# Attention's scores all beside the projections, its last values between the state space's scans, and GpSimd's products given to VectorE

## The chip, the cores and the metric

The kernel runs on one core of a Trainium2 chip. The metric is the time of one execution on the device, in microseconds, as the median of several runs.

A core has engines that each run their own instructions in order and wait for one another by semaphores: TensorE (PE, matrix products and transposes, into eight PSUM banks), VectorE (DVE, elementwise work, reductions and scans), ScalarE (ACT, activations and copies), GpSimd (POOL) and SyncE (SP, which here issues most DMAs).

## The reference

One decoder layer on a sequence of 1024 tokens with 1024 channels, in float32. Three parts follow each other, each with an RMSNorm ahead and behind, and a shift, scale and gate from a conditioning vector: half a SwiGLU step, token mixing, half a SwiGLU step. The change touches mixing alone:

```python
def sliding_window_attention(q, k, v, sinks):      # 8 query heads, 2 key heads, blocks of 128
    ...                                            # each block reads its own and the previous key block
    scores = einsum('bnqkgd,bnjkd->bnkgqj', qb, kk) * HEAD_DIM ** -0.5
    scores = where(valid, scores + bias, -inf)
    m = maximum(max(scores, axis=-1), sink)
    p = exp(scores - m)
    p = p / (sum(p, axis=-1) + exp(sink - m))
    out = einsum('bnkgqj,bnjkd->bnqkgd', p, vv)
    ...
def s5_ssm(u, a_re, a_im, log_step, b_re, b_im, c_re, c_im, d_skip, w_glu, b_glu):
    ...
    _, states = lax.associative_scan(combine, (a, bu), axis=1)   # complex diagonal state
    y = real(einsum('bsgp,ghp->bsgh', states, c_mat)) + u * d_skip
    y = gelu(y)
    y = y * sigmoid(y @ w_glu + b_glu)
    ...
```

The normed input is projected by w_in to q, k, v (attention, 512 channels) and u (state space, 512 channels). The outputs of both, each normed, are projected together by w_out.

## The kernel before, in words

Products of float32 matrices are made of three matmuls in a shorter format (`mm3`, L72 to L76): the high part of each side by the high part of the other, and the high parts by the low ones. `split` (L67 to L70) makes the parts: a cast by ACT (L69) and a subtraction by VectorE (L70).

PSUM banks of the mixing stage are handed out in turn, `b0` to `b7` (`mb`): an instruction that writes a bank waits until the last reader of what stood there before is done. The high and low parts of the transposed probabilities rotate over `h0` to `h7` (`o_rot`). In the listings below the names are tiles without that number, and behind them the number of the use: `b_1133` is a tile of the program, here in some bank.

The whole body stands in a context that gives the order of each engine's instructions by a schedule of its own (`TileContext(nc, schedule_with_timeline_sim=True)`), so the order on an engine follows the order in the code loosely. On an engine, the order is then fixed.

Mixing has twelve projection steps s = 0 to 11: four by `project` (the q, k and v columns that are left), then eight by `project_u`, one for each block of 128 tokens, 24 matmuls each (L919 to L921) and four copies by ACT (L923). Between them attention is threaded in: `at(n)` does three pieces of attention that belong to three blocks, `at_values(n - 3)`, `at_turn(n - 2)` and `at_scores(n)`. The table `AT` (L702) says behind which steps an `at` stands.

- `at_scores(t)`: two pairs of PSUM banks get the products of queries and keys (L831). VectorE adds the bias and takes the maximum (L841), ACT exponentiates (L848, L850, eight heads), VectorE sums, inverts and scales (L851, L852, L854, eight rows of work).
- `at_turn(t)`: TensorE transposes the probabilities (L865), `split` makes high and low parts from the banks (L69, L70).
- `at_values(t)`: `mm3` with the values (two groups of six matmuls, one group of three for block 0), ACT squares and copies the result out of its bank (L880, L882), VectorE sums the squares (L884), a matmul with ones sums over the heads (L886), VectorE copies that (L887).

Then u is transposed to `ug` (L949, copies by ACT at L950), and the state space runs over four groups of channels, q = 0 to 3. `ss_load(q)` fetches operands. `ss_state(q)` makes the input products (L968, 16 matmuls), scales and sums them on VectorE (L976 to L981), runs two scans along time (L982, L983), and turns the states back by three elementwise products and sums each for the real part (on VectorE, L993 to L995) and the imaginary one (the same lines, on POOL). The scans' decay factors are laid out by a POOL copy (L973). `ss_out(q)` makes the outputs (L1006, L1010), a Gelu on ACT (L1013), and transposes back (L1017, L1019). `out_a(t)` (L1038) is attention's share of w_out's product for block t, 24 matmuls. It needs `mix_a`, the split attention output, and the scale `rstd_a` (L1047). `more(n)` does one further `at(n)` between the state space's steps, and after the last one loads w_out's operands and makes `mix_a`.

Of the kernel before, what the change touches and what calls it, by code (L numbers as in the profile page):

```python
# [11 lines left out]
F32R = mybir.dt.float32r  # L12
# [3 lines left out]
MUL, ADD, SUB, MAX, MIN = ALU.mult, ALU.add, ALU.subtract, ALU.max, ALU.min  # L16

P = 128
D = 1024
NK = 8  # L20
NT = 8
# [9 lines left out]
def tile_layer(ctx: ExitStack, tc: tile.TileContext, a: dict, out: bass.AP, stage: str = "all"):  # L31
    nc = tc.nc
    pe, act, dve, pool, sp = nc.tensor, nc.scalar, nc.vector, nc.gpsimd, nc.sync
# [10 lines left out]
    def slot(tag, shape, dt=F32):  # L44
        uid[0] += 1
        return sb.tile([P] + list(shape), dt, tag=tag, name=f"{tag}_{uid[0]}")
# [5 lines left out]
    def small(n, name):  # L52
        uid[0] += 1
        return sm.tile([P, n], F32, tag=f"s_{name}_{n}", name=f"s{uid[0]}")
# [13 lines left out]
    def split(hi, lo, src, eng=dve):  # L68
        act.copy(hi, src)  # L69
        eng.tensor_tensor(lo, src, hi.bitcast(F32), op=SUB)  # L70
# [38 lines left out]
    r8 = cp.tile([P, 16], F32, name="r8")  # L109
    rstd_a, rstd_s, ss_a = (cp.tile([P, 8], F32, name=x) for x in ("rstd_a", "rstd_s", "ss_a"))  # L110
# [27 lines left out]
    def rsqrt(v, n):  # L138

        s, y = small(n, "rss"), small(n, "rsy")  # L140
        act.activation(s, v, AF.Sqrt)
        dve.reciprocal(y, s)
        dve.scalar_tensor_tensor(s, y, -0.5, y, op0=MUL, op1=MUL)
        dve.tensor_tensor(s, s, v, op=MUL)
        dve.scalar_tensor_tensor(y, s, 1.5, y, op0=ADD, op1=MUL)
        return y

    def rstd_of(ss, n, count):

        v = small(n, "rsv")  # L150
        dve.tensor_scalar(v, ss, 1.0 / count, EPS, op0=MUL, op1=ADD)
        return rsqrt(v, n)
# [546 lines left out]
        return todo  # L699


    AT = (1, 1, 0, 1, 0, 1, 0, 1, 0, 1, 0, 1)  # L702


    mb = Rot(*names("b", *range(8)))
# [48 lines left out]
    def mix(hm, st, st_u, late, shares, todo, start):  # L754
# [62 lines left out]
        ag = [slot(f"r{m}", [D]) for m in range(4)]  # L817
# [71 lines left out]
        def ss_load(q):  # L889
            e = slot(f"q{q % 2}", [4, 2, P])  # L890
            tw = slot(f"q{2 + q % 2}", [2, 512])
            f = slot(f"q{4 + q % 2}", [2, 4, P])
            tt = slot(f"q{6 + q % 2}", [8, P])
            sp.dma_start(e, e_d[q])
            sp.dma_start(tw, tw_d[q])
            for j in range(8):
                src = kp_d[q * P : (q + 1) * P, 112 - 16 * j : 240 - 16 * j].rearrange("(g h) w -> h g w", g=8)
                sp.dma_start(tt[16 * j : 16 * j + 16], src)
            sp.dma_start(f, f_d[q])
            B[q] = dict(e=e, tw=tw, f=f, t=tt)  # L900


        def at(n):

            if 3 <= n < NT + 3:
                at_values(n - 3)
            if 2 <= n < NT + 2:
                at_turn(n - 2)
            if n < NT:
                at_scores(n)  # L910
# [14 lines left out]
        n = 0  # L925
        for s in range(12):
# [6 lines left out]
            else:  # L933
# [3 lines left out]
                project_u(s - 4)  # L937
            if AT[s]:
                at(n)
# [19 lines left out]
        W = [slot(t, [2, 512]) for t in names("a", 4, 5, 6)]  # L959

        def ss_state(q):
            b = B[q]
            pp = [bank(mb(), [4, P]) for _ in range(2)]
            for g in range(4):
                for gp in range(2):
                    rows = slice(64 * gp, 64 * gp + 64)
                    for ri in range(2):
                        pe.matmul(pp[ri][rows, g, :], b["e"][:, g, ri, rows], ug[q][:, 2 * g + gp, :], start=True, stop=True)  # L968
            cs, sn = b["tw"][:, 0], b["tw"][:, 1]
            ir, ii = (p_.rearrange("p g c -> p (g c)") for p_ in pp)  # L970
            w1, w2, w3, w4, w5, w6 = (x[:, i] for x in W for i in range(2))
            dc = w5.rearrange("p (g c) -> p g c", g=4)
            pool.tensor_copy(dc, r8[:, 4 * q : 4 * q + 4].unsqueeze(2).broadcast_to([P, 4, P]))  # L973
            pool.memset(dc[:, :, 0], 0.0)

            dve.tensor_tensor(w1, ir, cs, op=MUL)  # L976
            dve.tensor_tensor(w2, ii, sn, op=MUL)
            dve.tensor_tensor(w1, w1, w2, op=ADD)
            dve.tensor_tensor(w3, ii, cs, op=MUL)
            dve.tensor_tensor(w4, ir, sn, op=MUL)  # L980
            dve.tensor_tensor(w3, w3, w4, op=SUB)  # L981
            dve.tensor_tensor_scan(w2, w5, w1, 0.0, op0=MUL, op1=ADD)  # L982
            dve.tensor_tensor_scan(w4, w5, w3, 0.0, op0=MUL, op1=ADD)  # L983

            hh = slot(("a8", "a9")[q % 2], [2, 4, P])
            hr, hi = hh[:, 0], hh[:, 1]

            def v3(x):
                return x.rearrange("p (g c) -> p g c", g=4)[:, :, 0 : P - 1]

            for dst, (p0, p1), op in ((hr, (cs, sn), SUB), (hi, (sn, cs), ADD)):
                eng, u1, u3 = (dve, w1, w3) if dst is hr else (pool, w5, w6)
                eng.tensor_tensor(u1, w2, p0, op=MUL)  # L993
                eng.tensor_tensor(u3, w4, p1, op=MUL)
                eng.tensor_tensor(dst[:, :, 1:P], v3(u1), v3(u3), op=op)  # L995
                pool.memset(dst[:, :, 0], 0.0)
            b["h"] = (hr, hi)

        def ss_out(q):
            b = B.pop(q)  # L1000
            yn = slot("a7", [8, P])
            py = [bank(mb(), [4, P]) for _ in range(2)]
            for g in range(4):
                for gp in range(2):
                    gr = 2 * g + gp
                    pe.matmul(py[gp][:, g, :], ug[q][:, gr, :], b["t"][:, gr, :], start=True, stop=False)  # L1006
                for ri in range(2):
                    for gp in range(2):
                        rows = slice(64 * gp, 64 * gp + 64)
                        pe.matmul(py[gp][:, g, :], b["h"][ri][rows, g, :], b["f"][rows, ri, g, :], start=False, stop=ri == 1)  # L1010
            for gp in range(2):
                dst = yn.rearrange("p i (g b h) -> p b g i h", g=4, b=2)[:, gp]
                act.activation(dst, py[gp].rearrange("p g (i h) -> p g i h", i=8), AF.Copy if stage == "ypre" else AF.Gelu_apprx_tanh)  # L1013
            for ih in range(2):
                pt = bank(mb(), [4, P])
                for i in range(4):
                    pe.transpose(pt[:, i, :], yn[:, 4 * ih + i, :], ident)  # L1017
                dst = y_t[q].rearrange("p (t i l) -> p t i l", t=8, i=8)[:, :, 4 * ih : 4 * ih + 4, :]
                act.copy(dst, pt.rearrange("p i (t l) -> p t i l", t=8))  # L1019
# [10 lines left out]
        def out_a(t):  # L1030
            acc.append(slot(("r1", "r2", "r3", "a14", "a15", "a4", "a5", "a6")[t], [D]))
            tk = slice(t * P, (t + 1) * P)
            for dh in range(2):
                dk = slice(dh * 512, dh * 512 + 512)
                pb = bank(mb())
                for m in range(4):
                    mm3(pb, mix_a[0][m][:, tk], mix_a[1][m][:, tk], wo[m][0][:, dk], wo[m][1][:, dk], m == 0, m == 3)
                dve.tensor_scalar(acc[t][:, dk], pb, rstd_a[:, t : t + 1], None, op0=MUL)  # L1038

        wo, mix_a = [], []  # L1040

        def more(n):
            if n < NT + 3:
                at(n)
            if n == NT + 2:
                late.load(1)
                dve.tensor_copy(rstd_a, rstd_of(ss_a, 8, 512))  # L1047
                mix_a.extend([slot(f"a{16 + 4 * i + m}", [D], F32R) for m in range(4)] for i in range(2))
                for m in range(4):
                    split(mix_a[0][m], mix_a[1][m], ag[m])  # L1050
                wo.extend(late.get(i) for i in range(4))
            return n + 1

        ss_load(1)
        n = more(n)
        ss_state(0)
        n = more(n)
        ss_state(1)
        n = more(n)
        ss_out(0)  # L1060
        ss_load(2)
        n = more(n)
        ss_state(2)
        n = more(n)
        ss_out(1)
        ss_load(3)
        while n < NT + 3:
            n = more(n)
        ss_state(3)
        out_a(0)  # L1070
        out_a(1)
        ss_out(2)
        y_split(0)
        y_split(1)
        out_a(2)
        out_a(3)
        ss_out(3)
        for t in range(4, 8):
            out_a(t)
        y_split(2)  # L1080
        y_split(3)
# [32 lines left out]
        wo = [shares.get(i) for i in range(4)]  # L1114
# [306 lines left out]
    w1 = Weights(a["w1_gu"], names("a", 4, 5, 6, 7), dve)  # L1421
# [109 lines left out]
    ins, us, late, shares = mix_streams()  # L1531
# [147 lines left out]
```

## Time and profile before

| | before |
|---|---|
| median of 3 runs | 1693.89 us (1691.98 to 1694.91) |
| profiled execution | 1698.31 us, span 1696.4 us |
| mean granted TensorE clock | 0.987 |
| PE busy | 1650.6 us, 97% of the span |
| VectorE, ACT, POOL busy | 74%, 47%, 6% of the span |

The span is the profiled part of one execution, the 1698.31 us are its whole time. "Busy" counts an engine's instructions without waits. The clock is the share of full speed that TensorE was granted; a matmul at half clock counts as busy twice as long. Mixing takes up the stretch from about 700 to 1050 us.

### The profile page before, as it was taken

The numbers are of one execution on the slowest core, as the hardware profiler recorded it, in microseconds if no ns is written. First come the engines' busy times: TensorE is split into PE (matmuls) and PEld (weight loads), VectorE is DVE, ScalarE is ACT, GpSimd is POOL, SyncE is SP. The second block draws the span as 40 slices with busy tenths as digits, with TensorE's granted clock in tenths as the row PEclk, the third lists the DMA queues.
The fourth block names the chain that finished last, engine by engine and source line by source line (L and its number), as shares of the span: only waits on it lengthen the run. The fifth ranks groups of instructions, "written<-read, shape, count | busy, mean of one in ns | idle before, by whom it ended". The sixth has DMA issues, their size and how long they took to land.

```text
span 1696.4 us, 22121 instructions
## 1 busy us (share of the span) xinstructions
PE 1650.6 (97%) x7669; PEld 1354.7 (80%) x7669; DVE 1254.8 (74%) x2407; ACT 802.4 (47%) x1650; POOL 107.8 (6%) x139
## 2 busy tenths in 40 slices
PE   5999999999999999999989998999999999999998
PEld 4888888787788888888767876878888888888886
DVE  7999997788869668746489368877665666679585
ACT  4633333553344467835564257633333333354462
POOL 0011100001100000000013053000000000000000
PEclk8999999999999999999979998999999999999999
DMA  9176752234496434430323126253322233493344
GB/s 376 47 273 229 252 185 94 106 131 151 140 346 212 118 111 164 173 112 13 111 77 88 50 96 201 75 188 113 112 94 93 94 109 122 161 364 109 111 131 142
DMA packets 110913, 249.07 MB, mean 147 GB/s; under 512 B 11961, under 2 KB 27617, under 8 KB 110801
## 3 DMA queue, kind: packets, MB, share of 16 engines
q1 hardware_dynamic: 101072, 214.12, 36.8%
q0 software_dynamic: 9152, 32.49, 5.8%
q8 instruction: 60, 0.98, 0.2%
q10 hardware_dynamic: 576, 1.05, 0.2%
q14 instruction: 53, 0.43, 0.1%
HBM read 187.87 MB, written 59.75 MB: 146 GB/s over the span
## 4 chain that ended last, share of the span: by engine, by line
PE 86%; DVE 7%; ACT 3%; issue 1%; DMA 1%; POOL 0%; SPq 0%; DVEq 0%; ACTq 0%; POOLq 0%
PE b L76 26%; PE b L75 26%; PE b L74 26%; PE b L831 1%; PE b L919 1%; PE b L921 1%; PE b L1010 1%; PE b L920 1%; PE b L865 1%; DVE a L70 1%; DVE w L70 1%; DVE h L485 1%; PE b L1006 1%; DMA r<-in_w_gu 1%; PE b L207 1%
## 5 line engine op out<-in xcount | busy, mean ns | idle before, releaser
L75 PE MATMUL b<-a,w 128*128 128x512 f32 x1260 | 493.1, 391 | 5.1 <-DVE a L70 5.1
L74 PE MATMUL b<-a,w 128*128 128x512 f32 x1260 | 490.1, 393 | 5.2 <-ACT a L69 2.4
L76 PE MATMUL b<-a,w 128*128 128x512 f32 x1260 | 493.0, 391 | 1.0 <-DVE w L70 0.8
L74 PEld LDWEIGHTS b<-a,w 128*128 128x128 f32 x1260 | 237.9, 189 | 58.1 <-ACT h L526 3.8
L75 PEld LDWEIGHTS b<-a,w 128*128 128x128 f32 x1260 | 237.8, 189 | 55.8 <-DVE a L70 6.6
L76 PEld LDWEIGHTS b<-a,w 128*128 128x128 f32 x1260 | 237.8, 189 | 52.2 <-DVE w L70 2.9
L70 DVE TENSOR_TENSOR w<-r,w 128x512 fp32r<-128x512 f32 (+1 forms) x206 | 142.8, 694 | 130.1 <-ACT w L69 129.8
L75 PE MATMUL b<-w,r 128*128 128x512 f32 x528 | 205.4, 389 | 0.0
L76 PE MATMUL b<-w,r 128*128 128x512 f32 x528 | 205.4, 389 | 0.0
L74 PE MATMUL b<-w,r 128*128 128x512 f32 x528 | 183.5, 389 | 0.0
L69 ACT CAST w<-r 128x512 fp32r<-128x512 f32 (+1 forms) x210 | 130.2, 623 | 94.1 <-DVE r L390 82.6
L69 ACT CAST r<-a 128x512 fp32r<-128x512 f32 x110 | 68.5, 623 | 146.1 <-PE b L76 105.8
L70 DVE TENSOR_TENSOR r<-a,r 128x512 fp32r<-128x512 f32 x110 | 75.6, 687 | 74.6 <-ACT r L69 74.5
L74 PEld LDWEIGHTS b<-w,r 128*128 128x128 f32 x528 | 99.1, 188 | 20.7
L76 PEld LDWEIGHTS b<-w,r 128*128 128x128 f32 x528 | 99.1, 188 | 20.5
L75 PEld LDWEIGHTS b<-w,r 128*128 128x128 f32 x528 | 99.1, 188 | 20.5
L69 ACT CAST w<-t 128x512 fp32r<-128x512 f32 (+1 forms) x114 | 69.9, 613 | 79.3 <-DVE t L393 31.7
L70 DVE TENSOR_TENSOR w<-t,w 128x512 fp32r<-128x512 f32 (+1 forms) x114 | 77.7, 682 | 36.0 <-ACT w L69 35.9
L522 DVE TENSOR_TENSOR h<-h,b 128x512 f32<-128x512 f32 x120 | 82.1, 684 | 20.5 <-PE b L76 18.7
L510 ACT ACTIVATE h<-h 128x512 f32<-128x512 f32 x60 | 38.0, 633 | 117.7 <-DVE h L522 117.7
L70 DVE TENSOR_TENSOR w<-a,w 128x512 fp32r<-128x512 f32 x110 | 75.1, 683 | 0.0
L74 PE MATMUL b<-a,a 128*128 128x512 f32 x182 | 72.0, 397 | 0.4 <-ACT a L69 0.4
(379 smaller groups left out, 2525.4 us busy)
## 6 DMA issues: line engine op xcount, KB each, us to landing
r<-in_w_gu SPq DMA_DIRECT2D x88, 512.0 KB, 4.2
g_d<-h SPq DMA_DIRECT2D x154, 256.0 KB, 2.2
a<-g_d SPq DMA_DIRECT2D x110, 256.0 KB, 2.8
q<-in_w_ada POOLq DMA_DIRECT2D x48, 512.0 KB, 4.6
a<-in_w_d SPq DMA_DIRECT2D x88, 256.0 KB, 5.4
a<-in_w_ada SPq DMA_DIRECT2D x24, 512.0 KB, 9.8
a<-in_x SPq DMA_DIRECT2D x12, 512.0 KB, 6.9
x_d<-a SPq DMA_DIRECT2D x12, 512.0 KB, 3.6
```

What stands on the lines that cost most here:

```text
L69: act.copy(hi, src)
L70: eng.tensor_tensor(lo, src, hi.bitcast(F32), op=SUB)
L74: pe.matmul(psum, wh, xh, start=first, stop=False, skip_group_check=goes_on)
L75: pe.matmul(psum, wh, xl, start=False, stop=False, skip_group_check=goes_on)
L76: pe.matmul(psum, wl, xh, start=False, stop=last, skip_group_check=goes_on)
L207: pe.matmul(pt[:, kk, :], xk, scale, start=True, stop=True)
L485: dve.tensor_tensor(d, x, y, op=op)
L510: act.activation(dst, src, AF.Silu)
L522: dve.tensor_tensor(dst, dst, pb, op=ADD)
L831: pe.matmul(pb[kv][:, m % 2, ks], qT[m][rows, t * P : (t + 1) * P], kT[rows, (t + 1 - nk) * P : (t + 1) * P], start=True, stop=True,)
L865: pe.transpose(pt[:, m, :], pr[4 * kv + m][:, b * P : (b + 1) * P], ident)
L919: pe.matmul(pb, hh, wh, start=k == 0, stop=False)
```

## The change

The table `AT` gets eight ones for seven, so that at(7), the last with scores, stands beside the projections too. In two places two `at` have only one projection between them. The three last `at`, which have no scores left, stand behind `ss_state(0)`, `ss_state(1)` and `ss_out(0)`. The split of attention's output and w_out's operands follow at once, behind `ss_load(2)`, w_out's loads are issued right behind `ss_load(1)`, and the shares `out_a(0)` to `out_a(4)` stand between the remaining steps of the state space, where two of them stood behind `ss_state(3)` and two behind `ss_out(2)`. `more` is gone.

In `ss_state` the imaginary part's two products and sum move from POOL to VectorE (they use the temporaries of the real part), and the layout of the decay factors moves from POOL to ACT. POOL keeps the memsets. One line is gone there, so the lines behind it have numbers smaller by one in the changed kernel: the products and sum are L992 to L994.

```diff
-    AT = (1, 1, 0, 1, 0, 1, 0, 1, 0, 1, 0, 1)
+    AT = (1, 1, 0, 1, 1, 0, 1, 0, 1, 1, 0, 1)
...
-            w1, w2, w3, w4, w5, w6 = (x[:, i] for x in W for i in range(2))
+            w1, w2, w3, w4, w5 = [x[:, i] for x in W for i in range(2)][:5]
             dc = w5.rearrange("p (g c) -> p g c", g=4)
-            pool.tensor_copy(dc, r8[:, 4 * q : 4 * q + 4].unsqueeze(2).broadcast_to([P, 4, P]))
+            act.copy(dc, r8[:, 4 * q : 4 * q + 4].unsqueeze(2).broadcast_to([P, 4, P]))
             pool.memset(dc[:, :, 0], 0.0)
...
             for dst, (p0, p1), op in ((hr, (cs, sn), SUB), (hi, (sn, cs), ADD)):
-                eng, u1, u3 = (dve, w1, w3) if dst is hr else (pool, w5, w6)
-                eng.tensor_tensor(u1, w2, p0, op=MUL)
-                eng.tensor_tensor(u3, w4, p1, op=MUL)
-                eng.tensor_tensor(dst[:, :, 1:P], v3(u1), v3(u3), op=op)
+                dve.tensor_tensor(w1, w2, p0, op=MUL)
+                dve.tensor_tensor(w3, w4, p1, op=MUL)
+                dve.tensor_tensor(dst[:, :, 1:P], v3(w1), v3(w3), op=op)
                 pool.memset(dst[:, :, 0], 0.0)
...
-        def more(n):
-            if n < NT + 3:
-                at(n)
-            if n == NT + 2:
-                late.load(1)
-                dve.tensor_copy(rstd_a, rstd_of(ss_a, 8, 512))
-                mix_a.extend([slot(f"a{16 + 4 * i + m}", [D], F32R) for m in range(4)] for i in range(2))
-                for m in range(4):
-                    split(mix_a[0][m], mix_a[1][m], ag[m])
-                wo.extend(late.get(i) for i in range(4))
-            return n + 1
-
         ss_load(1)
-        n = more(n)
+        late.load(2)
         ss_state(0)
-        n = more(n)
+        at(n)
         ss_state(1)
-        n = more(n)
+        at(n + 1)
         ss_out(0)
+        at(n + 2)
         ss_load(2)
-        n = more(n)
+        dve.tensor_copy(rstd_a, rstd_of(ss_a, 8, 512))
+        mix_a.extend([slot(f"a{16 + 4 * i + m}", [D], F32R) for m in range(4)] for i in range(2))
+        for m in range(4):
+            split(mix_a[0][m], mix_a[1][m], ag[m])
+        wo.extend(late.get(i) for i in range(4))
         ss_state(2)
-        n = more(n)
+        out_a(0)
         ss_out(1)
         ss_load(3)
-        while n < NT + 3:
-            n = more(n)
+        out_a(1)
         ss_state(3)
-        out_a(0)
-        out_a(1)
+        out_a(2)
         ss_out(2)
         y_split(0)
         y_split(1)
-        out_a(2)
         out_a(3)
+        out_a(4)
         ss_out(3)
-        for t in range(4, 8):
+        for t in range(5, 8):
             out_a(t)
```

What this does to an engine's order is shown at two places. The first is TensorE behind the first two projections of u. Before, the scores of block 3 (banks `b_1133` to `b_1135`) follow the values of block 0 (`b_1114`, `b_1115`), which come behind both projections (`b_1111`, `b_1112`); the end of the second projection and what follows:

```order
L921 MATMUL b_1112_6861<-q_1105_6824,a_908_5724 128x512
L74 MATMUL b_1114_6891<-h_1090_6764,a_1010_6207 128x512
...
L865 MATMUL b_1127_6941<-ident,c_1072_6649 128x128 x2
L831 MATMUL b_1133_6953<-a_1004_6201,a_1006_6203 128x256
...
L831 MATMUL b_1135_6963<-a_1004_6201,a_1008_6205 128x256
...
L886 MATMUL b_1117_6911<-ones,t_1116_6909 128x1
L919 MATMUL b_1140_6997<-q_1069_6644,a_893_5709 128x512
```

Behind the change the values of block 0 (`b_1113`, `b_1114`) stand within the first projection (`b_1111`), and the scores of block 3 (`b_1132` to `b_1134`) ahead of the second projection (`b_1139`):

```order
L76 MATMUL b_1114_6871<-h_1093_6773,a_1011_6208 128x512
...
L921 MATMUL b_1111_6832<-q_1105_6824,a_908_5724 128x512
...
L865 MATMUL b_1126_6912<-ident,c_1072_6649 128x128 x2
L831 MATMUL b_1133_6925<-a_1004_6201,a_1006_6203 128x256
...
L831 MATMUL b_1134_6934<-a_1004_6201,a_1008_6205 128x256
...
L886 MATMUL b_1116_6882<-ones,t_1115_6880 128x1
L831 MATMUL b_1132_6924<-a_1004_6201,a_1006_6203 128x256
...
L865 MATMUL b_1146_7056<-ident,a_1095_6777 128x128 x2
...
L919 MATMUL b_1139_6968<-q_1069_6644,a_893_5709 128x512
```

So the matmuls of one projection no longer stand between block 2's scores and block 0's values. The second place is VectorE behind the input products of the state space's first group (`b_1281` and its neighbour before, `b_1283` and `b_1284` after). The L70 rows in it free and feed the transposed probabilities for the next values. Before:

```order
L978 TENSOR_TENSOR a_1247_7581<-a_1247_7581 128x512
L884 TENSOR_REDUCE t_1287_7774<-t_1284_7749 128x128
L981 TENSOR_TENSOR a_1248_7582<-a_1248_7582 128x512
L982 SCALAR_TENSOR_TENSOR a_1247_7581<-a_1249_7583,a_1247_7581 128x512
L887 COPY ss_a<-b_1288_7776 128x1
L983 SCALAR_TENSOR_TENSOR a_1248_7582<-a_1249_7583,a_1248_7582 128x512
L993 TENSOR_TENSOR a_1247_7581<-a_1247_7581,q_1228_7511 128x512
L851 TENSOR_TENSOR s_7689<-s_7689,s_7690 128x8
L994 TENSOR_TENSOR a_1248_7582<-a_1248_7582,q_1228_7511 128x512
L70 TENSOR_TENSOR h_1291_7785<-b_1289_7779,h_1290_7784 128x512
```

And after the change, where L992 and L993 are the two products:

```order
L982 SCALAR_TENSOR_TENSOR a_1274_7694<-a_1276_7696,a_1274_7694 128x512
L983 SCALAR_TENSOR_TENSOR a_1275_7695<-a_1276_7696,a_1275_7695 128x512
L852 RECIPROCAL s_7600<-s_7600 128x8
L992 TENSOR_TENSOR a_1274_7694<-a_1274_7694,q_1255_7624 128x512
L884 TENSOR_REDUCE t_1289_7778<-t_1286_7753 128x128
L993 TENSOR_TENSOR a_1275_7695<-a_1275_7695,q_1255_7624 128x512
L854 TENSOR_SCALAR a_1244_7576<-a_1244_7576,s_7600 128x256 x2
...
L854 TENSOR_SCALAR c_1245_7577<-c_1245_7577,s_7600 128x256 x2
L70 TENSOR_TENSOR h_1293_7789<-b_1291_7783,h_1292_7788 128x512
```

There the eight scalings of block 7's probabilities (L854) and the sum of squares (L884) stand between the scans and the first L70.

## The prediction, made before the changed kernel ran

> **What bounds the kernel now.** I read the page's busy times first, then the windows around the changed place, then the timelines of the engines there. The page's first part (busy us, share of the span, instructions):
>
> ```profile
> PE 1650.6 (97%) x7669; PEld 1354.7 (80%) x7669; DVE 1254.8 (74%) x2407; ACT 802.4 (47%) x1650; POOL 107.8 (6%) x139
> ```
>
> TensorE is busy for all but 1696.4 - 1650.6 = 45.8 us, so the time can fall only where PE is idle, or where its clock is low (a matmul at half clock is busy twice as long). The windows show where (span, then busy time of each engine, then the granted PE clock, DMA share, GB/s). The first row is the eight `project_u` steps, the second goes from their end to the first matmul of w_out; then come 10-us slices.
>
> ```profile
> 766.80:834.90 68.10, 67.08 (x327) 54.05 (x326) 34.53 (x123) 34.39 (x134) 0.99 (x6) 1.00 0.08 31
> 834.90:906.70 71.80, 66.19 (x431) 50.05 (x429) 58.72 (x128) 50.05 (x137) 11.70 (x14) 0.88 0.43 123
> 860.00:870.00 10.00, 7.20 (x54) 5.39 (x50) 10.00 (x24) 9.13 (x31) 0.06 (x1) 0.96 0.45 157
> 869.50:886.60 17.10, 15.22 (x45) 10.69 (x45) 16.21 (x30) 8.06 (x19) 5.95 (x5) 0.51 0.21 63
> 990.00:1000.00 10.00, 8.55 (x42) 6.67 (x42) 5.48 (x12) 4.37 (x7) 2.82 (x3) 0.95 0.03 10
> 1000.00:1010.00 10.00, 10.00 (x40) 8.11 (x40) 6.96 (x12) 2.58 (x6) 5.30 (x3) 0.88 0.05 20
> ```
>
> The projections are nearly dense: 68.10 - 67.08 = 1.0 us idle, full clock. The second stretch is not: 71.80 - 66.19 = 5.6 us idle, and 17.1 us at clock 0.51 with 15.22 us of busy PE in them, which at full clock is 15.22 x 0.49 = 7.5 us less. So 13.1 us is what can be gained there, and nearly nothing what can be gained among the projections. The change moves attention's work out of the second stretch, partly into the first.
>
> **Part A: scores earlier among the projections.** The new table puts two `at` steps with a single projection between them, twice: at(2), `project_u(0)`, at(3); and at(5), `project_u(5)`, at(6). How long these pieces are on PE (start, length, line, idle ahead):
>
> ```profile
> 766.85 0.50 PE L919 MATMUL b<-q,a 128*128 128x512 f32 x1
> 777.86 0.39 PE L74 MATMUL b<-h,a 128*128 128x512 f32 x1
> 798.21 1.91 PE L865 MATMUL b<-ident,a 128*128 128x128 f32 x16
> 800.04 1.99 PE L831 MATMUL b<-a,a 64*128 64x256 f32 x12
> 802.86 0.47 PE L919 MATMUL b<-q,a 128*128 128x512 f32 x1 [0.51 <-DVE h L70]
> 822.51 0.47 PE L919 MATMUL b<-q,a 128*128 128x512 f32 x1 [0.51 <-DVE h L70]
> ```
>
> From 766.85 to 777.86 PE does two projections, so one is 5.5 us (24 matmuls). A `at_turn` is 1.8 us, three pairs of scores 1.9. On ACT and VectorE at the same time, for block 2's softmax and block 0's values:
>
> ```profile
> 776.44 0.19 ACT L850 ACTIVATION_READ_ACCUMULATOR a<-a,s 128x1 f32 x1
> 778.74 0.59 ACT L880 ACTIVATE t<-b 64x512 f32<-64x512 f32 x1
> 779.23 0.74 ACT L882 COPY r<-b 64x128 f32<-64x128 f32 x4
> 777.09 2.19 DVE L854 TENSOR_SCALAR a<-a,s 128x256 f32<-128x256 f32 x8
> 780.62 1.05 DVE L884 TENSOR_REDUCE t<-t 128x128 f32<-128x512 f32 x1 [1.33 <-ACT t L880]
> 781.88 0.69 DVE L70 TENSOR_TENSOR h<-b,h 128x512 fp32r<-128x512 f32 x1 [0.21 <-ACT h L69]
> 782.49 0.47 DVE L841 CUSTOM_DVE_ANT_0 a<-b,a,sink 128x256 f32<-128x256 f32 x1
> ```
>
> Up to 766.85 the two orders are the same, and the exps end at 776.5 in both. After the change PE has only `project_u(0)` (5.5 us), the six matmuls of values(0) (1.4) and the 16 transposes (1.8) from there: it is done at 766.85 + 8.7 = 775.5. The next scores want the bank of values(0), which ACT squares and copies only behind the exps: 776.5 + 0.5 + 0.75 = 777.75, and the second bank 1.2 later. VectorE meanwhile must do the eight L854, to 779.2, then L884 to 780.2, two L841 (0.4 each) and one L70 (0.6), whose read frees the bank for `project_u(1)`: 781.65. Between 775.5 and 781.65 PE has 2.35 us of work (six score matmuls of two records, L886, four transposes). So 6.15 - 2.35 = **+3.8 us** idle that `project_u(1)` covered before. It isn't repaid later, since the projections have only 1.0 us of idle.
>
> The second double costs less. The last pair of block 5's scores (`b_1193`) stands amid values(3), so block 5's exps run behind the casts of block 4's turn, and then L854 x8 stands ahead of the L70 that the next projection waits for. Summing the same durations along the new order I get waits of 0.6, 0.8, 0.1 and 1.5 us, **+2.4** (0.6 at L831 `b_1221`, 0.1 at the first transpose, and so on up to L919). The L919 waits of 0.51 at 802.86 and 822.51 go, since those places now have another order: **-1.0**.
>
> A stall may also halve the clock. In before, these gaps did:
>
> ```profile
> 866.94 0.38 PE L886 MATMUL b<-ones,t 128*128 128x1 f32 x2 [0.86 <-DVE t L884]
> 869.27 0.80 PE L74 MATMUL b<-h,a 128*128 128x512 f32 x1 [1.94 <-ACT h L69]
> 870.25 0.80 PE L74 MATMUL b<-h,a 128*128 128x512 f32 x1 [0.18 <-ACT h L69]
> 871.72 0.80 PE L75 MATMUL b<-h,a 128*128 128x512 f32 x1 [0.68 <-DVE h L70]
> 875.24 0.79 PE L75 MATMUL b<-h,a 128*128 128x512 f32 x1 [1.02 <-DVE h L70]
> 996.50 1.05 PE L1134 MATMUL b<-ones,a 128*128 128x1 f32 x8 [1.03 <-POOL a L1110]
> ```
>
> Two gaps of 0.86 and 1.94 within 3 us were followed by half clock at 869.5 to 886.6; a gap of 1.03 by a granted 0.88 in the slice 1000:1010 and 0.95 in the one before, 10 x (0.12 + 0.05) = 1.7 us lost. The stall here is 3.8 us in some 6, larger than both, so I add the smaller of the two prices, **+1.7**; the larger would be as much as after 875.24, some 11 us at half clock, 5.6 lost. For the second double I add none: its longest gap is 1.5 us and the 0.51 at 802.86 halved nothing; its bounds are 0 and 5.6.
>
> [...]
>
> **Part B: GpSimd's three products to VectorE, its copy to ACT.** Rows of POOL by line, and of VectorE and PE in block 0's state:
>
> ```profile
> L993 POOL TENSOR_TENSOR a<-a,q 128x512 f32<-128x512 f32 x4 | 7.5, 1874 | 49.3 <-DVE a L983 35.1 <-issue 14.2
> L973 POOL COPY a<-r 128x512 f32<-128x512 f32 x4 | 2.8, 698 | 4.5 <-PE b L920 4.3
> 862.72 0.68 DVE L976 TENSOR_TENSOR a<-b,q 128x512 f32<-128x512 f32 x1
> 864.07 1.27 DVE L731 SCALAR_TENSOR_TENSOR a<-a,cols,a 128x1024 fp32r<-128x1024 f32 x1
> 867.40 1.22 DVE L982 TENSOR_TENSOR_SCAN a<-a,a 128x512 f32<-128x512 f32 x1
> 872.25 1.75 DVE L995 TENSOR_TENSOR a<-a,a 128x508 f32<-128x508 f32 x1
> 900.45 0.67 DVE L995 TENSOR_TENSOR a<-a,a 128x508 f32<-128x508 f32 x1
> ```
>
> VectorE gets 12 more of 0.67, of which consecutive ones start 0.6 apart: 12 x 0.6 = 7.2 us. It loses the drag beside GpSimd (L995 took 1.75 there and 0.67 alone): 1.1 for each such overlap, 2 seen. So about 5 us more on an engine that is busy 58.72 of 71.80 us here. Ahead of PE it matters only where PE waits for a scan's result; counted with part C. ACT gets four copies of 0.6 (as L880); block 0's stands among `project_u`'s copies, which nobody waits for at once: 0, and at most 0.6 each.
>
> **Part C: scans, last values and w_out's shares.** The order still runs into a wait behind block 0's state (L968). On VectorE the first L976 is followed by three more products, an L731, two sums, two scans, L992, L884, L993 and eight L854 before the L70 `h_1293` that values want: 4 x 0.6 + 1.2 + 2 x 0.6 + 2 x 1.15 + 0.6 + 0.95 + 0.6 + 2.1 + 0.6, with two short ones of 0.1 each, 12.2 us. PE has 7.2 us in that time. It waits 1.05 at L886 and then 3.2 at the L75 with `h_1293`: 4.25 us, as against 4.7 now (0.86, 1.94, 0.18, 0.68, 1.02). The 5 us of VectorE's new work are in this chain with L993 (0.6) alone; the rest lies behind it. Later the casts of `mix_a` and the last L70 ahead of out_a(0) take 0.8, and Gelu's row 0.5. Idle: 5.6 us, no better than before's 5.6.
>
> What does improve is what comes after: no second gap like the one of 875.24, which in before kept the clock down 11.3 us longer (to 886.6). After 3.2 us idle I take 8 us at half clock, between 3.4 (half clock after 996.50, 1.7 lost by the slices) and 11.3; that is 4.0 lost, for 7.5. So the stretch costs 5.6 + 4.0 = 9.6 after 13.1: **-3.5**, with bounds 0 and -6 from the clock alone, and -11.8 if the wait goes too. Beyond it out_a(0..4) fills the later scans with 24 matmuls each, and PE waits for nothing that it doesn't wait for now; w_out's transfers (`late.load(2)`) start earlier on SP, in 8% DMA share, for which I count 0.
>
> **Sum.** +3.8 + 1.7 + 2.4 - 1.0 - 3.5 = +3.4 us. The profiled execution took 1698.31 us, 4.4 over the median of 1693.89; the difference is carried to the median: **1697.3 us**. A measurement of this kernel tells 0.2%, 3.4 us, from no change, so the forecast lies right on that bound.
>
> **Rivals.**
> 1. Clock unmoved by the doubles, and one 3.4-us piece at half clock behind block 0's scan: for it speaks that 0.51-us waits halved nothing; against it the 0.86 and 1.94. Then 3.8 + 2.4 - 1.0 - (13.1 - 5.6 - 1.7) = -0.6: 1693.3.
> 2. Faster: the wait behind block 0's state goes. The place is VectorE's chain of 12.2 us against PE's 7.2; it decides where VectorE has its four products and the scans done some 4 us earlier against PE, which happens if PE arrives that much later than I have it. Then no half clock either: 3.8 + 1.7 + 2.4 - 1.0 - 11.8 = -4.9: 1689.0. VectorE at 10.00 of 10.00 us in 860:870 speaks against.
> 3. Slower: the clock stays low behind both doubles as behind 875.24: 5.6 in place of 1.7, and 3.7 at the second: +3.4 + 3.9 + 3.7 = +11.0: 1704.9; behind one of them alone, 1701.
> 4. The change doesn't do what it says: at(7)'s scores still stand behind the last projection, beside the transposes of `ug`, and the wait behind block 0's scan is kept, so nothing is bought with the doubles' stalls, and those may be filled by what I take as dependent: about 1694.
>
> **How the numbers follow.** Forecast 0.38, its own range 1694.5 to 1700, half of it to each side of the bound. Rival 1: 0.20; rival 2: 0.14; rival 3: 0.20; rival 4: 0.08. Slower by over 0.2%: 0.19 + 0.20 and a little of rival 4, 0.41; faster (below 1690.5): 0.14 and a little of rival 1, 0.17; within: 0.42. The range leaves out half of rivals 2 and 3 each, 0.17: 1689.0 to 1703.5.
>
> **What would show it.** In the changed kernel's timeline: PE idle 3 to 4 us between the first two projections, released by ACT L882 and VectorE L884, L70; about 2.4 us around at(6), L831 and L919 named; one wait of about 3 us at L75 released by VectorE L70 behind block 0's scan; the granted clock from the projections' end to the first w_out matmul at 0.93 rather than 0.88. POOL's rows of L993 to L995 gone, and VectorE's at 0.67 all. The prediction is wrong if the window of the projections stays within 2 us of 68.10 for the same work (A fails), or if the stretch behind has under 3 us idle (C fails).

## The result: 0.7% slower, and the profile after

The changed kernel takes 1705.07 us (median, 1704.08 to 1705.95), the kernel before in the same comparison 1693.56 us. The ratio is 1.0070, with a 95% interval of 1.0058 to 1.0082: 11.5 us slower. The forecast was 1697.3 us with a range to 1703.5, so the direction that it leaned to was right and the size was not; rival 3 (1704.9 us) came nearest.

In the first part of the changed kernel's page PE's sum is 6.0 us higher than before, of the 6.6 us by which the span grew (1696.4 to 1703.0), so nearly all of the loss stands there as busy time and not as idle time (46.4 us after, 45.8 before). POOL's sum falls from 107.8 to 85.6 us, the others hardly change:

```profile
PE 1656.6 (97%) x7669; PEld 1358.7 (80%) x7669; DVE 1256.2 (74%) x2419; ACT 805.6 (47%) x1654; POOL 85.6 (5%) x123
```

TensorE's timeline of the changed kernel has the waits where they were expected (last column: idle ahead, and what ended it):

```profile
777.74 2.40 PE L831 MATMUL b<-a,a 64*128 64x256 f32 x8 [1.84 <-ACT r L882]
783.21 0.78 PE L919 MATMUL b<-q,a 128*128 128x512 f32 x1
837.85 3.06 PE L831 MATMUL b<-a,a 64*128 64x256 f32 x8 [1.54 <-DVE ss_a L887]
877.05 0.38 PE L886 MATMUL b<-ones,t 128*128 128x1 f32 x2 [0.71 <-DVE t L884]
880.35 0.79 PE L75 MATMUL b<-h,a 128*128 128x512 f32 x1 [2.92 <-DVE h L70]
```

The second projection starts at 783.21; in before it followed the first without a gap. The windows show what came behind each wait (span, busy PE, PEld, DVE, ACT, POOL, then the granted clock):

```profile
775.50:787.30 11.80, 9.71 (x32) 6.84 (x31) 8.39 (x28) 6.17 (x24) 0.00 (x0) 0.72 0.01 1
780.40:787.20 6.80, 6.80 (x20) 5.08 (x20) 4.67 (x17) 1.32 (x3) 0.00 (x0) 0.52 0.00 1
836.00:845.50 9.50, 7.96 (x25) 5.95 (x24) 8.50 (x33) 5.36 (x20) 0.00 (x0) 0.64 0.00 1
838.60:845.40 6.80, 6.80 (x19) 4.95 (x18) 6.36 (x23) 2.68 (x8) 0.00 (x0) 0.51 0.00 1
879.60:886.40 6.80, 6.05 (x19) 4.83 (x20) 6.80 (x12) 1.95 (x7) 0.00 (x0) 0.51 0.09 25
767.00:1001.85 234.85, 226.45 (x1210) 179.48 (x1208) 150.16 (x329) 121.20 (x323) 13.71 (x20) 0.96 0.23 72
```

Half clock came three times in this stretch, 6.8 us long each time. In the first, products of 512 columns (L919 to L921) start 0.43 us apart, from 784.21 to 787.20, and 0.23 apart at the full clock behind it. From the first projection of u to L1124 (the sums of squares of the state space's output, L1134 in before) the same work took 234.85 us; in before it took 229.65, from 766.85 to 996.50, so 5.2 us less. The rest of the program grew by 1.4 us only.

### The profile page after: what moved, and what is told of

The parts are those of the page before. It is cut to its first block, busy times and chain, and to the rows that moved or that the text cites. A ratio compares the mean times of both kernels' runs of the same rounds, so it can differ in the third digit from the quotient of the medians.

```text
span 1703.0 us, 22120 instructions
## 1 busy us (share of the span) xinstructions
PE 1656.6 (97%) x7669; PEld 1358.7 (80%) x7669; DVE 1256.2 (74%) x2419; ACT 805.6 (47%) x1654; POOL 85.6 (5%) x123
## 4 chain that ended last, share of the span: by engine, by line
PE 85%; DVE 7%; ACT 4%; DMA 2%; issue 1%; POOL 0%; SPq 0%; DVEq 0%; ACTq 0%; POOLq 0%
PE b L75 26%; PE b L76 26%; PE b L74 26%; PE b L831 1%; PE b L919 1%; PE b L921 1%; PE b L1009 1%; PE b L920 1%; DVE a L70 1%; DVE w L70 1%; DVE h L485 1%; PE b L865 1%; DMA r<-in_w_gu 1%; PE b L1005 1%; PE b L207 1%
## 5 line engine op out<-in xcount | busy, mean ns | idle before, releaser
L75 PE MATMUL b<-a,w 128*128 128x512 f32 x1260 | 493.2, 391 | 5.2 <-DVE a L70 5.2
L75 PEld LDWEIGHTS b<-a,w 128*128 128x128 f32 x1260 | 237.9, 189 | 55.9 <-DVE a L70 6.6
L70 DVE TENSOR_TENSOR w<-r,w 128x512 fp32r<-128x512 f32 (+1 forms) x206 | 142.9, 694 | 130.0 <-ACT w L69 129.7
L75 PE MATMUL b<-w,r 128*128 128x512 f32 x528 | 205.4, 389 | 0.0
L70 DVE TENSOR_TENSOR r<-a,r 128x512 fp32r<-128x512 f32 x110 | 75.7, 688 | 74.7 <-ACT r L69 74.7
L75 PEld LDWEIGHTS b<-w,r 128*128 128x128 f32 x528 | 99.1, 188 | 20.5
L70 DVE TENSOR_TENSOR w<-t,w 128x512 fp32r<-128x512 f32 (+1 forms) x114 | 77.8, 683 | 35.0 <-ACT w L69 34.9
L70 DVE TENSOR_TENSOR w<-a,w 128x512 fp32r<-128x512 f32 x110 | 75.3, 684 | 0.0
L75 PE MATMUL b<-a,a 128*128 128x512 f32 x182 | 72.1, 396 | 0.0
```

Source lines behind the costliest of these rows:

```text
L75: pe.matmul(psum, wh, xl, start=False, stop=False, skip_group_check=goes_on)
```

## The experiments

The first theory was that the two doubles of the table (two `at` with a single projection between them) cost the time, by waits and the half clock behind them. Its rival laid the loss on the work behind the projections, above all on VectorE's added products. A second theory came with the results: what follows a stall sets how long half clock lasts.

**The kernel before once more** (no edit).

> The kernel before, unchanged. Its profiled execution took 1698.31 us, 4.4 over its median of timed runs. Theory 1: that execution was an odd one, and the 4.4 us lie in the state space's stretch, where half clock lasted 17.1 us: a second profile shows about half of that (3.4 to 9 us of half clock, 1.7 to 4.5 us lost) and a total near 1694. Rival: every profiled execution is 4 us longer; then the new profile again shows 17 us of half clock there and about 1698 us.

1692.88 us (the profiled execution 1693.36). The waits behind the first scan are the same to 0.01 us, the half clock after them is not:

```profile
868.50:878.70 10.20, 7.69 (x17) 4.98 (x18) 10.20 (x21) 6.40 (x16) 5.95 (x5) 0.51 0.25 80
875.11 0.80 PE L75 MATMUL b<-h,a 128*128 128x512 f32 x1 [1.02 <-DVE h L70]
991.63 1.05 PE L1134 MATMUL b<-ones,a 128*128 128x1 f32 x8 [0.30 <-POOL a L1110]
```

10.2 us against 17.1. L1134 starts at 991.63 here, 4.9 us earlier than in the profile that the prediction was worked from. So that profile held about 5 us that a usual execution of the kernel doesn't have. The expectation of 3.4 to 9 us was passed by 1.2; that every profile is 4 us longer is ruled out.

**The new table alone**, in the kernel before:

```diff
-    AT = (1, 1, 0, 1, 0, 1, 0, 1, 0, 1, 0, 1)
+    AT = (1, 1, 0, 1, 1, 0, 1, 0, 1, 1, 0, 1)
```

> The kernel before with the new table AT alone (at(8) to at(10) then stand behind ss_load(1), ss_state(0) and ss_state(1); GpSimd keeps its part, w_out's shares stay where they were). Theory 1, the two doubles of the table cost the time, 3.6 us idle and 6.7 us at half clock among the projections: 1701 to 1705 us, with the waits at L831 at about 777 and 837 us in its trace and half clock behind both. Rival, the loss comes from VectorE's added products and the new order behind the projections: 1692 to 1696 us.

1709.26 us, ratio 1.0093 (1.0078 to 1.0108): more than the whole change. The two waits stand where they were said to stand:

```profile
776.90 2.40 PE L831 MATMUL b<-a,a 64*128 64x256 f32 x8 [2.11 <-ACT r L882]
837.02 3.05 PE L831 MATMUL b<-a,a 64*128 64x256 f32 x8 [1.54 <-DVE ss_a L887]
875.30 1.98 PE L968 MATMUL b<-a,q 128*64 128x128 f32 x16 [1.96 <-ACT a L950]
906.68 2.39 PE L968 MATMUL b<-a,q 128*64 128x128 f32 x18 [2.32 <-ACT a L1019]
```

That the state space now has less attention beside it shows too: its own products wait for ACT's copies (the last two rows). The doubles lose time without any of the rest, though not all of these 16.2 us are theirs; the rest, taken with them, gives 4 us back.

**The first double alone**, `AT = (1, 1, 0, 1, 1, 0, 1, 0, 1, 0, 1, 0)` in the kernel before, with seven steps as there.

> The kernel before with AT = (1, 1, 0, 1, 1, 0, 1, 0, 1, 0, 1, 0): seven steps beside the projections as before, but with the first double, at(2), project_u(0), at(3); nothing else changed. Theory 1, the first double alone costs some 3.5 us of waits and 6.8 us at half clock, less the 0.51 us wait that goes: 1699 to 1703 us. Rival, a double matters only where all eight scores have to fit: 1692 to 1696 us.

1700.81 us, ratio 1.0053 (1.0040 to 1.0065), 7.5 us. The wait is there, 6.8 us at clock 0.51 behind it, and no other among the projections:

```profile
778.13 3.34 PE L831 MATMUL b<-a,a 64*128 64x256 f32 x8 [1.97 <-ACT r L882]
779.20:786.00 6.80, 6.66 (x18) 4.71 (x18) 6.33 (x20) 2.88 (x9) 0.00 (x0) 0.51 0.00 1
```

**VectorE instead of ACT for the values of blocks 0 and 3**, in the changed kernel:

```diff
             for kv in range(2):
...
+                if t in (0, 3):
+                    for m in range(4):
+                        dve.tensor_copy(ag[m][rows, tk], po[rows, m, :])
+                        dve.tensor_tensor(sq[rows, m], ag[m][rows, tk], ag[m][rows, tk], op=MUL)
+                    continue
                 act.activation(sq[rows], po[rows], AF.Square)
```

> The changed kernel, in which VectorE rather than ACT squares and copies the values of blocks 0 and 3 out of their banks, the two that stand one projection behind another block's scores. Theory 1, the first waits of both doubles come from ACT's order (exps ahead of those copies): the L831 waits at about 777 and 838 us shrink below 0.8 us, fewer pieces of half clock follow, 1696 to 1702 us. Rival, VectorE's scalings and L70 hold TensorE there anyway, and get longer by 3 us: 1704 to 1709 us.

1702.01 us, 3.1 less than the changed kernel and just past the range of the first theory, which had asked for both waits below 0.8 us. The first wait fell from 1.84 to 0.85 us and half clock did not follow it (granted clock 1.00 from 766.8 to 799.0); a shorter one (3.4 us) came later, behind other waits, and the second double was unmoved (1.38 us, 6.8 us at half clock). So ACT's order is part of the first wait, as the walk had it, and not of the second.

**Three other tables** in the changed kernel, all eight steps beside the projections.

> The changed kernel with AT = (1, 1, 1, 0, 1, 0, 1, 0, 1, 1, 0, 1): all eight steps beside the projections, the first double taken apart (at(2) a step earlier, at(3) behind project_u(0) with two projections ahead of it), the second double kept. Theory 1, each double costs its own wait and its own pieces of half clock: the wait at 777 us is gone, the one at L831 near 837 us stays, and the time is that of the changed kernel less 4 to 6 us, 1699 to 1701 us. Rival, the waits only move with all scores squeezed in: 1703 to 1707 us with some L831 wait elsewhere.

> The changed kernel with AT = (1, 1, 1, 0, 1, 0, 1, 0, 1, 0, 1, 1): at(2) a step earlier, and the one pair of steps with a single projection between them at the very end (at(6), project_u(7), at(7)). Theory 1: no wait of over 1 us among the projections but at their end, so 1693 to 1698 us, faster than the changed kernel by 7 to 12. Rival, the pair at the end costs what the double did and the half clock then lasts on through the small transposes of u: 1699 to 1705 us.

> The changed kernel with AT = (1, 1, 1, 1, 0, 1, 0, 1, 0, 1, 0, 1): at(2) and at(3) both among the first four steps, with one projection between them as in the first double, and the old spacing behind. Theory 1, a wait for exps and copies wherever values(0) stand one projection behind block 2's scores: a wait of 1.5 to 2 us at L831 ahead of project_u(0), half clock of 3.4 to 6.8 us behind it, and none in the second half: 1698 to 1702 us. Rival, the first steps have room: no wait there, 1692 to 1697 us.

They gave 1715.86, 1706.39 and 1699.70 us. The first two failed in both theories' terms. With at(2) one step earlier in the code, block 2's scores did start earlier on TensorE (758.91 in the second kernel, 765.09 in the changed one), but its exps did not: ACT ran them up to 775.3 us, against 776.5 in the changed kernel, still right ahead of block 0's values, and the wait stood (the second kernel's):

```profile
776.60 3.39 PE L831 MATMUL b<-a,a 64*128 64x256 f32 x12 [1.44 <-ACT r L882]
```

So their doubles were not taken apart, and they price nothing. The first kernel's 10.8 us over the changed one go with a longer stretch of half clock behind the scans, whose cause is open:

```profile
894.00:918.50 24.50, 24.50 (x103) 18.50 (x103) 10.74 (x14) 8.15 (x15) 0.24 (x3) 0.51 0.33 92
```

In the third, only four of block 3's twelve score records stand ahead of `project_u(0)` on TensorE. The scheduler put the other eight within `project_u(1)`:

```profile
770.97 1.13 PE L831 MATMUL b<-a,a 64*128 64x256 f32 x4
772.15 0.50 PE L919 MATMUL b<-q,a 128*128 128x512 f32 x1
780.08 1.13 PE L831 MATMUL b<-a,a 64*128 64x256 f32 x4
781.57 1.13 PE L831 MATMUL b<-a,a 64*128 64x256 f32 x4
```

There was room, as its rival said: no wait of over 0.51 us among the projections, and full clock (the third kernel's window, 93.2 us):

```profile
766.80:860.00 93.20, 92.04 (x467) 70.57 (x466) 53.96 (x187) 55.58 (x200) 0.38 (x5) 1.00 0.19 54
```

That is the changed kernel with the waits and the half clock of both doubles gone: 5.4 us faster than it. It is still slower than before (1.0031, 1.0019 to 1.0042), so the time lies in the first theory's range and not in the rival's, though the half clock behind the scans lasts 10.2 us, as in the second profile of the kernel before. Where these 5 us lie was not settled.

**The change with the old table**, with at(7) behind `ss_load(1)`:

> The changed kernel with the old table AT (at(7) then stands behind ss_load(1)). Theory 1: the projections are dense again (about 1 us idle, full clock), and the time is 1690 to 1696 us. Rival, the rest of the change is what costs: 1700 to 1706 us.

**Only GpSimd's part given to VectorE and ACT**, in the kernel before:

> The kernel before with only GpSimd's products given to VectorE and its copy to ACT. Theory 1: 1692 to 1696 us, since VectorE's added 7.2 us lie beside TensorE's work but for one product. Rival, VectorE was the limit of that stretch (58.7 us busy of 71.8): 1698 to 1702 us.

1700.05 us (1691.72 to 1709.80) and 1700.55 us (1688.82 to 1702.30). Both medians lie in the rivals' ranges, the first at its very edge, so the rest of the change does cost time without the doubles. The parts don't add up: the table alone costs 16.2 us, the rest alone 7.0, and both together 11.5. The cause that the second rival named isn't seen, though. The projections are dense in both (67.08 us busy of 68.10 in the first, two waits of 0.51 us in the second), and behind the first scan the waits sum to some 4.4 us, against 4.7 before; a new one of 1.54 us stands ahead of it, at the L968 of the first group. What differs most is the half clock that follows, 27.2 us in both profiles (the first row is the change with the old table), with TensorE busy for nearly all of it:

```profile
870.10:897.30 27.20, 25.21 (x94) 19.91 (x95) 20.76 (x38) 13.10 (x34) 0.14 (x2) 0.50 0.29 83
872.40:899.60 27.20, 26.21 (x97) 20.81 (x98) 20.33 (x35) 12.11 (x30) 0.14 (x2) 0.50 0.30 92
```

The times of one and the same kernel spread over 13 to 18 us here, and the mean granted clock of an execution goes with its time: 0.992 at 1691.72 us and 0.980 at 1709.80 in the first, 0.992 at 1688.82 and 0.983 at 1702.30 in the second. So the amount of half clock differs between executions; where in them it lies is known for the profiled ones alone. Why it is usually longer in these two kernels than before stays open.

**GpSimd's part given back**, in the changed kernel:

> The changed kernel with GpSimd's three products and copy given back to it. Theory 1, that part moves nothing on the path to the L75 that waits behind the first scan but one product of 0.6 us: 1702 to 1706 us. Rival, VectorE's added work is part of the loss: under 1701 us.

1704.34 us, as the first theory said: in the changed order this part is worth nothing that shows in the time. In the trace it does move the path to that L75. Beside GpSimd's products two of VectorE's scalings took 2.69 us, and the wait behind them 5.54 us in place of 2.92 (two rows of this run, then the same scalings in the changed kernel):

```profile
877.96 2.69 DVE L854 TENSOR_SCALAR a<-a,s 128x256 f32<-128x256 f32 x2
883.29 0.80 PE L75 MATMUL b<-h,a 128*128 128x512 f32 x1 [5.54 <-DVE h L70]
877.50 0.62 DVE L854 TENSOR_SCALAR a<-a,s 128x256 f32<-128x256 f32 x2
```

So the time was right and the theory's reason was not. The profiled execution is 2.0 us longer than that of the changed kernel (1706.76 to 1704.76). The other three have a mean granted clock of 0.989, against 0.984 to 0.985 in the changed kernel's, so less half clock makes up for the longer wait in the median.

**Where half clock ends.** Half clock lasted 3.4 us in the kernel with VectorE's values, 6.8 at each double, 17.1 and 10.2 in the two profiles of the kernel before, and 27.2 in the change with the old table and with GpSimd's part alone: each close to a whole number of pieces of 3.4 us. I moved `ss_out(0)` behind the next `more(n)`, so that values' 512-column products would come first:

```diff
-        ss_out(0)
-        ss_load(2)
         n = more(n)
+        ss_out(0)
+        ss_load(2)
         ss_state(2)
```

> The kernel before with ss_out(0) and ss_load(2) behind the next more(n), so that 512-column products of values stand nearer to the stall behind the first scan and fewer 128-column ones of ss_out. Theory 2, the half clock after a stall lasts in whole pieces of 3.4 us until a piece has enough 512-column work, and the small products of ss_out do not count as enough: the 10 to 17 us at half clock there become 3.4 to 7, and the time 1689 to 1692 us. Rival, the length depends on the gaps alone: the same as before, 1692 to 1695 us.

> The same move of ss_out(0) in the kernel before with GpSimd's part given to VectorE and ACT (which alone gave 1688.8 to 1702.3 us, with 27.3 us at half clock in its profile). Theory 2: half clock there 3.4 to 7 us, 1688 to 1693 us, without the runs at 1700. Rival: 1699 to 1702 us as it was.

1708.48 and 1712.89 us: both theories' numbers were passed, by 10 us and more. In the first kernel half clock did end, but new waits of 1.32 and 1.22 us stood ahead of the now longer run of small products, and it came back for 20 us. In the profile of the second kernel (1721.17 us, its longest execution, 8 us over its median) it lasted 58 us, and in most of that TensorE waited for nothing:

```profile
884.10:903.50 19.40, 19.39 (x59) 14.20 (x58) 14.17 (x19) 8.77 (x17) 0.10 (x1) 0.50 0.17 55
903.50:928.50 25.00, 25.00 (x123) 20.40 (x122) 11.46 (x22) 8.18 (x12) 0.38 (x5) 0.50 0.32 84
928.50:940.00 11.50, 11.50 (x56) 9.62 (x55) 8.83 (x13) 1.08 (x2) 0.00 (x0) 0.98 0.17 46
```

The last row begins where the first 512-column products of w_out start, at 928.55. But the clock was full again from 928.9 (last row below), so what ran ahead of that was mostly small products:

```profile
921.86 1.22 PE L1009 MATMUL b<-q,a 64*128 64x128 f32 x4
923.01 0.79 PE L1005 MATMUL b<-q,a 128*128 128x128 f32 x2
923.73 1.22 PE L1009 MATMUL b<-q,a 64*128 64x128 f32 x4
924.88 3.73 PE L968 MATMUL b<-a,q 128*64 128x128 f32 x32
928.55 0.66 PE L74 MATMUL b<-a,a 128*128 128x512 f32 x1
928.90:940.00 11.10, 11.10 (x54) 9.27 (x54) 8.58 (x13) 1.08 (x2) 0.00 (x0) 1.00 0.11 41
```

L1005 and L1009 have six records in 1.9 us, L968 has 32 in 3.7 us, all of 128 columns. Then 24 useless products of 512 columns were put behind `ss_out(0)`, into that kernel and into the kernel before:

```diff
         ss_out(0)
+        pf = bank(mb())
+        for i in range(24):
+            pe.matmul(pf, v_hi[:, i % 8, :], v_hi[:, 0:4, :].rearrange("p a b -> p (a b)"), start=i == 0, stop=i == 23)
```

> The last kernel (ss_out(0) later, GpSimd's part given away; 58 us at half clock, 1712.9 us) with 24 added products of 512 columns behind ss_out(0), whose result nobody reads: 5.5 us of work at full clock, more at half. Theory 2, a piece with enough 512-column work ends the half clock and the small products behind it keep the full clock: half clock ends by about 912 us in place of 929, and the time is 1705 to 1713 us, in spite of the added work. Rival, the small products are slow for themselves, or the length of the half clock has another cause: it lasts as long as before, and the time is 1718 to 1724 us.

> The kernel before with the same 24 added products behind ss_out(0). There the clock is full again by 879 to 887 us, so they should cost their own time only: 5.5 us, 1698 to 1700 us, by both theories; less only where they shorten the half clock behind the first scan, by theory 2 at most by a piece of 1.7 us.

1712.26 us (1712.13 to 1712.66) and 1702.46 us (1699.21 to 1703.36). In the first the half clock ends inside the added products, 4.3 us after the first, and the small products behind run at full clock:

```profile
902.81 1.22 PE L1009 MATMUL b<-q,a 64*128 64x128 f32 x6
903.96 5.23 PE L1063 MATMUL b<-a 128*128 128x512 f32 x13
909.16 2.77 PE L1063 MATMUL b<-a 128*128 128x512 f32 x11
...
915.36 0.71 PE L1005 MATMUL b<-q,a 128*128 128x128 f32 x4
916.00 0.72 PE L1009 MATMUL b<-q,a 64*128 64x128 f32 x8
908.00:929.00 21.00, 21.00 (x171) 17.44 (x170) 16.72 (x29) 8.30 (x12) 0.24 (x3) 0.99 0.34 91
```

L1009 takes 1.22 us for six records at 902.81 and 0.72 for eight at 916.00. So the products are not slow for themselves, and half clock can end within 512-column work.

That such work is needed to end it is not shown, and the other traces speak against it. In the kernel before, the 17.1 us of half clock ended at 886.3, within transposes and small products and 8.8 us behind the last 512-column one:

```profile
877.11 0.63 PE L76 MATMUL b<-h,a 128*128 128x512 f32 x1
...
884.76 0.63 PE L865 MATMUL b<-ident,c 128*128 128x128 f32 x2
885.32 0.79 PE L1010 MATMUL b<-q,a 64*128 64x128 f32 x2
886.04 0.60 PE L1006 MATMUL b<-q,a 128*128 128x128 f32 x2
886.57 0.71 PE L1010 MATMUL b<-q,a 64*128 64x128 f32 x4
```

In the first kernel with `ss_out(0)` later it ended at 904.3, behind most of 32 records of L968 again. A guess that fits these ends is how closely products follow each other and not how wide they are; no run varied that alone.

The times don't show that the added products shorten half clock either. The median fell by 0.6 us against the kernel without them, but the granted clock of its other four executions was 0.981 to 0.984, and with them 0.981 to 0.982. In the kernel before the same products cost 8.8 us, more than the 5.5 expected, and its profile has 17 us of half clock behind the scan as well. Against the first profile of the kernel before, which had as much, it is 4.8 us longer (1703.08 to 1698.31). What the other 3 us are was not settled.

## Why the prediction was wrong

**First double: +3.8 and +1.7 forecast, 6.9 measured.** From the first L919 at 767.0 to the end of half clock at 787.2 TensorE did the first projection (5.45 us at full clock), six matmuls of values (1.36), 20 transposes (2.3), the scores (1.9), L886 (0.25) and nine matmuls of the second projection (2.0), 13.3 us in 20.2. The order of waits was as walked: exps to 776.5, L882, then VectorE's L854, L884, L841 and L70. The idle term holds, since 3.5 of the 6.9 us are waits (1.84 at the first L831, the rest between the scores and ahead of L919). The clock term failed: "I add the smaller of the two prices" put one piece of half clock, 1.7 us lost, where two came, 3.4 us lost.

**Second double: +2.4 forecast, 5.5 measured.** From L886 at 836.03 to 845.58, 4.0 us of full-clock work took 9.5. The waits were about right; the step that failed is "for the second double I add none", argued from a 0.51 us wait that halved nothing. A wait of 1.54 us was followed by two pieces again.

**The two L919 waits of 0.51 us** went, as said: -1.0.

**Behind the first scan: idle 4.25 forecast, 0.71 + 2.92 = 3.6 measured; half clock 8 us forecast, 6.8 measured.** The L884, L854, L70 order held TensorE as said. Against the profile before, the work up to L1124 took 5.2 us longer; take off 6.9 + 5.5 - 1.0 = 11.4, and this part with the rest of the stretch gave 6.2 back, for a forecast of 3.5. The reason given for the gain does not stand: the second gap, of 1.02 us at 875, is in both profiles of the kernel before, and half clock ended 11 us behind it in one and 3.8 in the other. So it need not have kept the clock down.

**The sum and what it was carried to.** Against the profiled execution the change cost 1704.76 - 1698.31 = 6.5 us, for +3.4 forecast; against the median 11.5. The other 5 us are the step "the difference is carried to the median". The 17.1 us of half clock in the profile before were its own: the second profile of the same kernel had 10.2. There the same work took 224.97 us (766.66 to 991.63), 9.9 less than in the changed kernel, so against that one this part gave back only 11.4 - 9.9 = 1.5 us. I had noted that the execution was 4.4 us over the median, and did not ask where those 4.4 us stood. They stood in the very place from which I took the gain.

**What was right:** the places and releasers of the waits, and about what half clock costs behind the first scan in this order (4.0 us forecast, 3.4 measured). The part from GpSimd was worth nothing in the time, as counted, but by luck: with it given back that wait is 2.6 us longer, through VectorE's scalings beside GpSimd's products, and only a higher granted clock makes that up in the median. Rival 3 had half clock at both doubles. Its price at the first, 5.6 us, was too high and at the second, 3.7, about right (3.4 measured for each). That its total came near is luck too: it counted a gain of 3.5 us behind the projections, of which 1.5 are left against a usual execution, and that made up for most of the high price at the first double.

**The clock.** How long a wait has to be before half clock follows was not shown. Waits of 1.84 and 1.54 us at the doubles were followed by it; one of 0.85 us (VectorE's values), those of 0.51 us among the projections before, and the 1.54 us at the first group's L968 in the change with the old table and in the kernel with GpSimd's part alone were not. What ends it was not shown either. In the profile with 58 us of half clock TensorE was busy for 44.39 of the 44.40 us from 884.1 to 928.5, and the clock stayed at 0.50; in the kernel before it ended at 886.3, 0.9 us behind a run of transposes (L865).

## What to carry to other kernels

Spacing mattered more than totals here: block 2's softmax took VectorE and ACT 11.6 us in the kernel before (767.67 to 779.28), and for the step behind it 5.5 us of projection were too few (a wait of 1.84 us) and 11 enough; one projection did where most of the next scores came within the projection behind it. My estimate from these numbers is that such a step should stand about as much matmul time behind the softmax as the softmax takes on both engines together. Price a stall on TensorE as its idle time plus the half clock behind it, in these profiles whole pieces of 3.4 us, and look at what follows it: at the doubles, with dense 512-column products behind the wait, it ended after two pieces, while with mostly small products behind it it lasted 58 us in one execution, though that these kept it up is not shown. And before a gain is read off one profiled execution, see whether its stretch is the one that makes that execution longer than the median.

## What the hardware showed that I had not expected

TensorE at clock 0.50 for 44 us (884.1 to 928.5, in the kernel with `ss_out(0)` later and GpSimd's part given away) while its busy time was all of that time, mostly with products of 64 and 128 rows and 128 columns; and 32 records of another 128-column product, close behind each other in 3.7 us, stood right ahead of its end. The kernel before had half clock behind the same waits for 17.1 us in one execution and 10.2 in another. No version that was tried beats the kernel before in the median; the least execution of all, 1688.82 us, belongs to the kernel with only GpSimd's part moved, whose median is 1700.55.
